# An encoder block on one core: attention is put into the same planned row of steps, and the same 51 buffers, as the rest

## The chip, the cores and the metric

The kernel runs on one core of a Trainium2 chip. The time is device microseconds of one execution. Five engines work side by side, each through its own instructions in order: PE (TensorE, matmuls; its weight loads are shown as PEld), DVE (VectorE), ACT (ScalarE), POOL (GpSimd) and SP (SyncE), which here issues nearly all DMAs. They wait for each other by semaphores.

## The reference, cut to what matters

One layer on x of 2048 tokens by 1024 features, all in float32:

```
h = rms_norm(x, norm1_g)
proj = h @ w_in                       # u, v | q, k, v | two gates of 1024
u, v = gelu(first 1024 columns)
y_a = u * (w_s @ layer_norm(v) + b_s)             # per chunk of 128 tokens, 4 groups
q, k = rms_norm(q, q_g) / 8, rms_norm(k, k_g)     # 8 heads of 64
# tokens are a grid of 32 rows x 64 columns; each query sees 8 rows x 16 columns
p = softmax(q . k_window + bias(na_rpb))
y_b = p @ v_window
merged = sigmoid(g1) * (y_a @ w_o_a) + sigmoid(g2) * (y_b @ w_o_b)
x = x + merged @ w_out
x = x + square(relu(rms_norm(x, norm2_g) @ w_ff1)) @ w_ff2
```

## The kernel before, in words

A float32 matmul is made of three fp32r matmuls: each operand is split into a high part (a cast on ACT, `t_hi`, `r_hi`, `w_hi`) and a low part (a subtraction on DVE, L1345, L1424). The large products go through a seven-product scheme (`seven` and `seven_tok`, L1452 and L682): sums of weight blocks are made on POOL (L1384 to L1391), sums of inputs on POOL too (`sums`, L415 to L428), and 7 steps of 12 matmuls of 128x512 replace 8.

The program has three parts, one behind the other, each with its own SBUF pool.

Part one, `first_steps` (L1054), is planned: `Plan` holds a list of PE steps and chains of stages on other engines (an SP load, a POOL sum, an ACT cast, a DVE subtraction, an SP store), each stage with a cost and a lead before the step that needs it. `Plan.run` goes through the steps once, keeps a model of each engine's clock and of 51 free buffers of 4 KB per partition, and writes every instruction in the order that it finds; the engines then follow this order. Part one makes u, the gates and then, in 16 slices of 128+128 tokens, v with the spatial gating (`values`, L701, 8 slices) and the queries and keys (`queries`, L822, 8 slices). What later steps need is stored to DRAM: `gt` (gates), `ut` (u), `ya`, `vs`, `qs`, `ks`. The input sums for the slices lie in DRAM as `xf`, laid out as [half, partition, 7 parts, 4, 512 tokens]; a slice reads 128 tokens of each, in runs of 512 bytes (L646). `bias_tables` (L977) builds the attention's bias in DRAM (`sk`, then nine tables `tb`) with DMAs and small operations on POOL; it is one chain, due at the end of part one.

Part two, attention (`attention`, L1243), is not planned: it is written out in program order with pools of its own, and a scheduler interleaves PE's work. There are 16 units (4 pairs of heads by 4 row blocks), each of 4 column blocks. For each of these 64 blocks PE makes the scores of two heads (L1177), DVE adds the bias and takes the maximum (L1184), ACT takes the exponential (L1187), DVE scales by the inverse sums (L1193), PE turns the result (L1206), DVE and ACT copy it (L1207, L1210), and PE multiplies by v (L1219). K is loaded from POOL's queue (`kst`, L1128), everything else from SP's. DVE reorders the queries (`q`, L1159). Between the blocks, 32 fillers (`branch_units`, L1276) multiply `ya` by w_o_a (L350, tiles `y`, `woa_hi`, `woa_lo`, `fg`), 12 matmuls of 128x512 each, times a gate `g` (L1306), stored as `ma`. Two fillers come ahead of attention, 24 within, 6 behind:

```
        with self.list_part():
            self.load_unit(0)
            units = self.branch_units()
            next(units)
            next(units)
```

Part three, `rest` (L1784), is planned by a second `Plan` with new buffers: the merge with w_o_b, w_out, and the two feed-forward products for each half of the tokens.

Of the kernel before, what the change touches and what calls it, by code (L numbers as in the profile page):

```python
# [19 lines left out]
P = 128  # L20
# [13 lines left out]
NRAW, NW, NACT, NBUF = 5, 12, 29, 51  # L34
# [209 lines left out]
class Block:  # L244


    def __init__(self, ctx, tc, a):
# [21 lines left out]
        self.xf = d("xf", [2, P, 7, 4, 512])  # L269
# [5 lines left out]

    def list_part(self):

        part = ExitStack()
        pool = lambda name, bufs: part.enter_context(self.tc.tile_pool(name=name, bufs=bufs, reuse_waits="tile"))
        self.slots = pool("slots", 1)  # L280
        self.half = pool("half", 5)
        self.ybp = pool("ybp", 1)
        return part
# [17 lines left out]
    def slot(self, shape, dt=F32, name="slot", tag="act"):  # L301
        return self.slots.tile([P] + shape, dt, tag=tag, name=name, bufs={"raw": NRAW, "w": NW, "act": NACT}[tag])

    def h512(self, dt=F32, name="half"):
        return self.half.tile([P, 512], dt, tag="half", name=name)

# [6 lines left out]

    def split(self, shape, src, name, pool=False):

        nc = self.nc
        hi = self.slot(shape, F32R, name + "_hi", "w")
        lo = self.slot(shape, F32R, name + "_lo", "w")
        if pool:
            nc.gpsimd.tensor_copy(hi, src)  # L320
            nc.gpsimd.tensor_tensor(lo, src, hi.bitcast(F32), ALU.subtract)
        else:
            nc.scalar.copy(hi, src)
            nc.vector.tensor_tensor(lo, src, hi.bitcast(F32), ALU.subtract)
        return hi, lo

    def load_raw(self, w, c0, ncol, nkt, name):

        per = 1024 // ncol
        raws = []  # L330
        for r0 in range(0, nkt * P, per * P):
            raw = self.slot([per, ncol], F32, name, "raw")
            self.nc.sync.dma_start(raw, w[r0 : r0 + per * P, c0 : c0 + ncol].rearrange("(k p) n -> p k n", p=P))
            raws.append(raw)
        return raws

    def load_wk(self, w, c0, ncol, nkt, name, pool=False):
        per = 1024 // ncol
        tiles = []
        for r0 in range(0, nkt * P, per * P):  # L340
            (raw,) = self.load_raw(w[r0 : r0 + per * P], c0, ncol, per, name)
            tiles.append(self.split([per, ncol], raw, name, pool))
        return lambda kt, hl: tiles[kt // per][hl][:, kt % per, :]
# [21 lines left out]
    def feat_gemm(self, w, m, X, nk=8):  # L365

        pt = self.ps("fg", "mm")
        ms = slice(m * P, (m + 1) * P)
        self.gemm(pt, [([w(k, 0)[:, ms], w(k, 1)[:, ms]], [X[k][:, 0], X[k][:, 1]]) for k in range(nk)])
        return pt  # L370


    def feat(self, h, xs, c0, row, act, dst, leads=(26, 15, 10)):
# [26 lines left out]
        for i, p in ((0, 2), (1, 4)):  # L400
            def out(i=i):
                nc.sync.dma_start(dst(i), e[i][1].rearrange("p b t -> p (b t)"))
                self.give(e[i][0])
            self.post(ids[p], [self.store(out, 1, 0)], 8)
# [44 lines left out]
    def norm_chain(self, e, name, i, k, acc, sq, after, width):  # L449
# [5 lines left out]
        def square():  # L455
# [4 lines left out]
            nc.scalar.activation(at(acc[0][1]) if k == 0 else at(sq[0][k % 2][1]), at(e[name][1]), AF.Square)  # L460
# [6 lines left out]
        return self.plan.chain([Stage("ACT", 0.1 + 0.5 * n, square, new, 0, 6, 0.3), Stage("DVE", 0.1 + 0.58 * n, add, 0, 0, 3, 0.3)], after)  # L467

    def first_u(self):
# [47 lines left out]
        for b in range(2):  # L517
# [47 lines left out]
            for _, st in fs:  # L565
                self.post(i, [self.store(st, 1, 0)], 2)
# [487 lines left out]
    def first_steps(self):  # L1054
# [28 lines left out]
        for c in range(2):  # L1083
            if c == 1:
                self.constants()
# [778 lines left out]
```

## Time and profile before

| what | value |
|---|---|
| median of 3 runs | 2811.0 us (2809.34 to 2811.19) |
| the profiled execution's own time | 2806.74 us |
| its span, first to last instruction | 2804.9 us |
| PE busy | 2561.2 us (91%) |
| DVE busy | 1857.1 us (66%) |
| ACT busy | 1159.6 us (41%) |
| POOL busy | 1105.1 us (39%) |
| mean granted clock of PE | 0.956 |
| DMA | 573.76 MB, mean 205 GB/s |

The span is the time of the program from its first to its last instruction; the runs' times hold about 2 us more. Busy shares are means over all stages. A table of stages (busy time of each engine, granted clock and DMA share in stretches of time) tells in which stages PE is not busy; the waits of that stage tell for whom. Stages of part one end near 880 us (start until 120, gates until 460, values until 640 and on to about 690, queries until 880), attention and its fillers run from 930 to 1231 us, and part three from there to the end.

### The profile page before, as it was taken

To read this page: it belongs to the slowest core of one execution; us is meant where nothing else is said; L and a number is where in the kernel's file an instruction comes from. 1 tells how busy PE (TensorE), PEld (TensorE's weight loads), DVE (VectorE), ACT (ScalarE), POOL (GpSimd) and SP (SyncE) were. 2 spreads that over 40 slices of the span, in tenths; PEclk is the share of its full clock that TensorE was granted. 3 is DMA by queue.
4 is the path that set the end of the run, shared out by engine and by line. 5 is a ranking of instruction groups with operands and counts; after the bars stand their busy time and mean duration, and the time that the engine had idled before them with its cause. 6 is when DMAs were issued, how large, how long until landed. Compare 5 with 4: busy or idle time off the path is not lost. (4 is left out here: it accounts for less than half of the span.)

```text
span 2804.9 us, 34089 instructions
## 1 busy us (share of the span) xinstructions
PE 2561.2 (91%) x11820; PEld 2071.9 (74%) x11820; DVE 1857.1 (66%) x2781; ACT 1159.6 (41%) x1802; POOL 1105.1 (39%) x800
## 2 busy tenths in 40 slices
PE   7799998779994799989998999989998999989999
PEld 5577887567773566668887888868886888868887
DVE  5667666547884477656376756588777666677776
ACT  5456545436542234423244443343333333443331
POOL 2553573540000111003334766634433666643441
PEclk9899999889997899999999999999999999989999
DMA  4467689989866999978766444474446444374442
GB/s 150 161 226 243 244 300 286 236 225 277 204 172 174 291 259 272 281 244 299 247 230 224 158 142 161 152 250 155 153 143 225 154 158 147 132 252 153 152 155 96
DMA packets 419164, 573.76 MB, mean 205 GB/s; under 512 B 33901, under 2 KB 283156, under 8 KB 418992
## 3 DMA queue, kind: packets, MB, share of 16 engines
q1 hardware_dynamic: 401600, 543.75, 60.8%
q0 software_dynamic: 13248, 27.82, 3.8%
q8 instruction: 93, 1.52, 0.2%
q10 hardware_dynamic: 4144, 0.02, 0.1%
q14 instruction: 79, 0.65, 0.1%
HBM read 368.45 MB, written 202.98 MB: 204 GB/s over the span
## 5 line engine op out<-in xcount | busy, mean ns | idle before, releaser
L1452 PE MATMUL z<-x_t,t_hi 128*128 128x512 f32 x1184 | 372.7, 396 | 39.4 <-DVE x L1768 28.2
L1345 DVE TENSOR_TENSOR r_lo<-w_r,r_hi 128x1024 fp32r<-128x1024 f32 (+3 forms) x176 | 286.3, 1628 | 82.0 <-ACT r_hi L1341 58.1
L1384 POOL TENSOR_TENSOR w_s<-w_r 128x512 f32<-128x512 f32 (+3 forms) x88 | 117.8, 1339 | 456.7 <-PE y L1452 261.2
L1452 PEld LDWEIGHTS z<-x_t,t_hi 128*128 128x128 f32 x1184 | 224.4, 191 | 92.2 <-DVE x L1768 10.3
L1452 PE MATMUL z<-x_t,t_lo 128*128 128x512 f32 x592 | 234.2, 396 | 1.5 <-DVE t_lo L1345 1.5
L1452 PE MATMUL x<-x_r,t_hl 128*128 128x512 f32 x888 | 219.7, 396 | 8.3 <-DVE x_r L1424 7.6
L1341 ACT CAST r_hi<-w_r 128x1024 fp32r<-128x1024 f32 (+3 forms) x176 | 173.7, 988 | 85.2 <-PE z L1452 62.7
L1452 PEld LDWEIGHTS x<-x_r,t_hl 128*128 128x128 f32 x888 | 169.9, 192 | 46.2 <-DVE x_r L1424 8.5
L1128 POOL DMA_DIRECT2D kst<-ks x32 | 26.5, 831 | 446.8 <-DMA ks<-qo 263.7
L1452 PE MATMUL z<-x_t,r_hi 128*128 128x512 f32 x592 | 183.6, 392 | 1.6 <-DVE x L1768 1.3
L1452 PE MATMUL z<-x_r,r_hi 128*128 128x512 f32 x592 | 183.9, 392 | 0.0
L1452 PE MATMUL y<-x_r,r_hi 128*128 128x512 f32 x592 | 183.6, 391 | 0.0
L1452 PE MATMUL x<-x_r,r_hi 128*128 128x512 f32 x592 | 182.2, 389 | 0.0
L1768 DVE TENSOR_TENSOR x<-z,x 128x512 f32<-128x512 f32 x152 | 104.8, 690 | 95.3 <-PE z L1452 95.3
L1420 ACT CAST x_r<-x_r 128x1024 fp32r<-128x1024 f32 x104 | 107.6, 1050 | 143.8 <-DVE t_hl L1345 99.9
L1391 POOL TENSOR_TENSOR w_s<-w_r,w_s 128x512 f32<-128x512 f32 (+3 forms) x88 | 151.3, 1719 | 37.0 <-DVE t_lo L1345 10.0
L1390 POOL TENSOR_TENSOR w_s<-w_r 128x512 f32<-128x512 f32 (+3 forms) x88 | 159.5, 1812 | 4.8
L350 PE MATMUL fg<-mg,w_hi 128*128 128x512 f32 x512 | 158.0, 389 | 0.9 <-DVE mg L1525 0.9
L1385 POOL TENSOR_TENSOR w_r<-w_r,w_r 128x512 f32<-128x512 f32 (+3 forms) x88 | 148.7, 1690 | 7.6 <-DMA w_r<-in_w_in_dram 0.6
L1345 DVE TENSOR_TENSOR t_lo<-w_s,t_hi 128x1024 fp32r<-128x1024 f32 (+3 forms) x88 | 136.2, 1548 | 16.6 <-ACT t_hi L1341 8.4
L1424 DVE TENSOR_TENSOR x_r<-x_r,x_r 128x1024 fp32r<-128x1024 f32 x104 | 138.7, 1352 | 3.5 <-ACT x_r L1420 3.5
L1420 ACT CAST x_t<-x_t 128x1024 fp32r<-128x1024 f32 (+1 forms) x104 | 84.6, 835 | 122.3 <-PE x L1452 80.6
(257 smaller groups left out, 6107.9 us busy)
## 6 DMA issues: line engine op xcount, KB each, us to landing
w_r<-in_w_ff_dram SPq DMA_DIRECT2D x116, 512.0 KB
x_r<-af SPq DMA_DIRECT2D x64, 512.0 KB
x_r<-xf SPq DMA_DIRECT2D x40, 512.0 KB
w_r<-in_w_in_dram SPq DMA_DIRECT2D x36, 512.0 KB
gt<-fe SPq DMA_DIRECT2D x32, 512.0 KB
qn<-qs SPq DMA_DIRECT2D x64, 256.0 KB
g<-gt SPq DMA_DIRECT2D x64, 256.0 KB
x<-x SPq DMA_DIRECT2D x32, 512.0 KB
```

The costliest lines, as they stand in the source:

```text
L350: self.nc.tensor.matmul(out, w[p], x[q], start=(i == 0 and j == 0), stop=(i == n - 1 and j == 2))
L1128: nc.gpsimd.dma_start(k.rearrange("p r c -> p (r c)"), self.ks[:, :, hd, pair, r0 * GW : (r0 + n) * GW].rearrange("l d t -> (l d) t"),)
L1341: nc.scalar.copy(e[name + "_"][1][0], e[name][1])
L1345: nc.vector.tensor_tensor(lo, e[name][1], hi.bitcast(F32), ALU.subtract)
L1384: nc.gpsimd.tensor_tensor(s23[:, :, 1], r1[:, :, 0], r1[:, :, 1], ALU.subtract)
L1385: nc.gpsimd.tensor_tensor(r1[:, :, 1], r1[:, :, 1], r2[:, :, 1], ALU.add)
L1390: nc.gpsimd.tensor_tensor(s23[:, :, 0], r1[:, :, 1], r1[:, :, 0], ALU.subtract)
L1391: nc.gpsimd.tensor_tensor(e["t4"][1], r2[:, :, 0], s23[:, :, 0], ALU.subtract)
L1420: nc.scalar.copy(hi, lo.bitcast(F32))
L1424: nc.vector.tensor_tensor(lo, lo.bitcast(F32), hi.bitcast(F32), ALU.subtract)
L1452: nc.tensor.matmul(out, a[u], b[v], start=(p in (1, 5, 2) and k == 0 and j == 0), stop=(k == n - 1 and j == 2), skip_group_check=p in (6, ...
L1768: nc.vector.tensor_tensor(v, bank, v, ALU.add)
```

## The change

All three parts become one plan. `list_part` and its pools go; `first_steps`, `attention` and `rest` add steps and chains to one `Plan`, with one set of 51 buffers, and `Plan.run` is called once. Attention's scores, turns and products are PE steps (`scores`, `turn`, `products`); block i's scores, then a filler if i is even, then block i-1's turn, then block i-2's products. Their loads are chains on SP, K's too. The query reorder is a POOL stage; the second head's scaling goes from DVE to ACT. The fillers go token block by token block with all of w_o_a held split (cast on ACT, subtraction on DVE) instead of column block by column block. Each load names the store that it comes after (`k_done`, `q_done`, `yb_done` and others). `bias_tables` starts behind the first steps and is due where the last gates begin. `xf` is laid out by token slices, so that a slice's two parts are one run of 4 KB; its stores and the second half's reload then go in runs of 512 bytes. The first 16 squares (`norm_chain`) go from ACT to POOL. Leads and costs of some stages get other numbers.

```diff
-        self.xf = d("xf", [2, P, 7, 4, 512])
+        self.xf = d("xf", [2, P, 4, 7, 4, P])
...
-            nc.scalar.activation(at(acc[0][1]) if k == 0 else at(sq[0][k % 2][1]), at(e[name][1]), AF.Square)
+            o, x = at(acc[0][1]) if k == 0 else at(sq[0][k % 2][1]), at(e[name][1])
+            if width == 512:
+                nc.gpsimd.tensor_tensor(o, x, x, ALU.mult)
+            else:
+                nc.scalar.activation(o, x, AF.Square)
...
-        return self.plan.chain([Stage("ACT", 0.1 + 0.5 * n, square, new, 0, 6, 0.3), Stage("DVE", 0.1 + 0.58 * n, add, 0, 0, 3, 0.3)], after)
+        return self.plan.chain([Stage("ACT" if n == 2 else "POOL", 1.3 if n == 1 else 1.1, square, new, 0, 6, 0.3), Stage("DVE", 0.1 + 0.58 * n, add, 0, 0, 3, 0.3)], after)
...
-        st += self.stores(e, ("w1", "w2", "t23", "t4"), self.xf[h][:, :, c], (True,) * 4)
+        def out(name, part):
+            def f():
+                p0, p1 = self.X_PART[part]
+                for p in range(p0, p1):
+                    v = e[name][1][:, p - p0] if p1 - p0 == 2 else e[name][1]
+                    nc.sync.dma_start(self.xf[h][:, :, p, c], v.rearrange("p (t q) -> p t q", q=P))
+                self.give(e[name][0])
+            return f
+
+        st += [Stage("SP", self.DMA, out(nm, p), 0, 1, 3 - 0.5 * i, 2.0) for i, (nm, p) in enumerate((("w1", "r1"), ("w2", "r2"), ("t23", "t23"), ("t4", "t4")))]
...
-                src = self.xf[h][:, p0:p1, :, t * P : (t + 1) * P] if n == 2 else self.xf[h][:, p0, :, t * P : (t + 1) * P]
+                src = self.xf[h][:, t, p0:p1] if n == 2 else self.xf[h][:, t, p0]
...
-            self.post(i, [self.store(out, 1, 0)], 6)
+            self.v_done[tok[0] // P] = self.v_done[tok[1] // P] = (self.post(i, [self.store(out, 1, 0, 5.0)], 6), 1)
...
+        start = len(plan.steps)
...
+            self.first_w(0, 2 + c, len(plan.steps) + 6)
...
-        plan.step(0.5, lambda: None)
-        end = plan.step(1.0, lambda: None)
-        self.bias_tables(mark, end)
-        plan.run()
...
+        self.bias_tables(start, end)
+
+
+    def unit(self, pair, rb):
+
+
+        nc, plan = self.nc, self.plan
...
+            def load_k(e=e, hd=hd):
+                e[0] = self.take([n, GW], F32R, "kst")
...
+            ks.append((e, plan.chain([Stage("SP", 1.6, load_k, 1, 0, 12, 3.0)], tuple(self.k_done[t] for t in rows), hold=(1, give))))
...
+            def order(e=e):
+                e[0] = self.take([4, 2, P], F32R, "q")
+                for cb in range(4):
+                    nc.gpsimd.tensor_copy(
+                        e[0][1][:, cb].rearrange("p l (r c) -> p (l r) c", c=16),
+                        e[1][1].rearrange("p l (r f c) -> p f (l r) c", f=4, c=16)[:, cb],
                     )
...
+            qs.append((e, plan.chain([Stage("SP", 1.8, load_q, 1, 0, 16, 3.0), Stage("POOL", 3.0, order, 1, 1, 6, 0.3)], tuple(self.q_done[t] for t in range(4 * rb, 4 * rb + 4)), hold=(1, give))))
...
+    def scores(self, pair, rb, cb, unit):
...
+        def first():
+            e["rec"] = self.sm(2, "rec")
+            nc.vector.reciprocal(e["rec"], e["sums"])
+            nc.vector.tensor_scalar(e["p"][1][:, 0], e["p"][1][:, 0], e["rec"][:, 0:1], None, ALU.mult)
+
+        def second():
+            nc.scalar.activation(e["p"][1][:, 1], e["p"][1][:, 1], AF.Copy, scale=e["rec"][:, 1:2])
...
+        i = plan.step(0.95 * u, prod, [c for _, c in ks + qs] + [bias[1]], evac, 1, {"DVE": 1.15 * u, "ACT": 0.8 * u})
+        ch = plan.chain([Stage("DVE", 0.15 + 0.5 * u, first, 0, 0, 1.5, 0.2), Stage("ACT", 0.1 + 0.5 * u, second, 0, 0, 0.8, 0.2)], start=i)
...
+        fills = self.branch_units()
+        done = 0
...
+                p[i] = self.scores(*todo[u], cb, units[u])
+            while done < 32 and done * 64 <= 32 * i:
+                next(fills)
+                done += 1
...
+                pT[i - 1] = self.turn(todo[u][1], cb, p.pop(i - 1))
...
+                s = self.products(todo[u][1], cb, units[u], pT.pop(i - 2), po, o)
...
+                ys.append((e, plan.chain([self.load(e, "y", [2, 512], self.ya[:, :, k, b * 512 : b * 512 + 512], 8, dt=F32R)],
+                                         tuple(self.ya_done[t] for t in range(4 * b, 4 * b + 4)), hold=(1, lambda e=e: self.give(e["y"][0])))))
...
+                    g = plan.chain([self.load(e, "g", [512], self.gt[at], 8)], (self.gt_done[b // 2, m],))
+                    i = plan.step(12 * self.MM, prod, [ws[c][1], g] + [y[1] for y in ys], evac, 0, {"DVE": 0.7})
+                    self.ma_done[m, b] = (self.post(i, [self.store(out, 1, 0, 1.0)], 6), 1)
...
-    def w_seven(self, w, k1, k2, c0, leads=(26, 15, 10)):
+    def w_seven(self, w, k1, k2, c0, leads=(22, 14, 9)):
...
-                [Stage("SP", self.DMA * n / 2, load, 1, 0, 14, 3.0),
+                [Stage("SP", self.DMA * n / 2, load, 1, 0, 11, 3.0),
...
-        with self.plan_part("one"), self.tc.manual_schedule():
+        with self.plan_part("buf"), self.tc.manual_schedule():
             self.first_steps()
-        with self.list_part():
-            self.units, self.bias = {}, {}
-            self.load_unit(0)
-            units = self.branch_units()
-            next(units)
-            next(units)
-            done = 2
-
-            def fill(step):
-                nonlocal done
-                while done < 26 and done < 2 + (step + 1) * 24 / 64:
-                    next(units)
-                    done += 1
-
-            self.att_queries(self.units[0])
-            self.attention(fill)
-            for _ in units:
-                pass
-        with self.plan_part("two"), self.tc.manual_schedule():
+            self.attention()
             self.rest()
```

The places where the order of instructions changes most are shown below as they stand in the two programs, without row numbers; names carry the buffer's number.

PE before, where the queries end and attention begins: `qT` turns the last slice's queries and keys, `fg` is a filler, `s` are scores.

```order
L893 MATMUL qT_6848<-ident_98,q_6626 128x128 x4
L893 MATMUL qT_6856<-ident_98,k_6666 128x128 x4
L350 MATMUL fg_6963<-y_6915,woa_hi_6949 128x512 x2
L350 MATMUL fg_6963<-y_6915,woa_lo_6950 128x512
...
L350 MATMUL fg_6980<-y_6921,woa_lo_6950 128x512
L350 MATMUL fg_7116<-y_6923,woa_hi_6949 128x512 x2
L350 MATMUL fg_7116<-y_6923,woa_lo_6950 128x512
L350 MATMUL fg_7116<-y_6925,woa_hi_6949 128x512 x2
L1177 MATMUL s_7008<-kst_6889,q_6995 128x264 x2
```

PE after, at the same place (L851 is the turn, L1154 the scores, L304 the filler, L1199 the turn of p):

```order
L851 MATMUL qT_6928<-ident_98,q_6676 128x128 x4
L851 MATMUL qT_6943<-ident_98,k_6721 128x128 x4
L1154 MATMUL s_6955<-kst_6635,q_6557 128x264 x2
L1154 MATMUL s_6958<-kst_6637,q_6694 128x264 x2
L304 MATMUL fg_6984<-y_6824,w_hi_6530 128x512 x2
L304 MATMUL fg_6984<-y_6824,w_lo_6531 128x512
...
L1154 MATMUL s_6998<-kst_6635,q_6557 128x352 x2
L1154 MATMUL s_7001<-kst_6637,q_6694 128x352 x2
L1199 MATMUL pTp_7015<-ident_98,p_6961 120x128 x2
```

Two whole fillers stood ahead of the first scores; now one filler stands behind them, and steps are whole groups.

SP before, behind the last stores of the queries (`qs`, `ks`); `woa` is the fillers' first weight load:

```order
L917 DMA qs_72<-qo_6853 64x8x128 x2
L915 DMA ks_73<-qo_6861 64x4x128 x4
L1135 DMA qn_6891<-qs_72 64x2x512 x2
...
L1118 DMA bias_6913<-tb20_88 128x2x264
L1284 DMA y_6915<-ya_79 128x2x512
L1284 DMA y_6917<-ya_79 128x2x512
```

SP after, there:

```order
L604 DMA x_t4_6407<-xf_93 128x512
L1369 DMA w_6409<-in_w_o_a_dram 128x4x256
L875 DMA qs_72<-qo_6425 64x8x128 x2
L1096 DMA qn_6507<-qs_72 64x2x512 x2
L873 DMA ks_73<-qo_6467 64x4x128 x4
L875 DMA qs_72<-qo_6510 64x8x128 x2
L873 DMA ks_73<-qo_6539 64x4x128 x4
L1096 DMA qn_6611<-qs_72 64x2x512 x2
L1084 DMA kst_6635<-ks_73 128x704
```

Before, all of the first unit's loads and then 16 loads of `y` stood behind the last store and ahead of `woa`; now the weights, queries and keys of the first unit stand among the stores of the last slices, and four `y` follow.

POOL before, where the bias tables follow the last sums of part one:

```order
L1391 TENSOR_TENSOR w_s4_3128<-w_r2_3030,w_s23_3106 128x512
...
L428 TENSOR_TENSOR t4_3242<-w2_3134,t23_3223 128x512
L987 MEMSET rpbv_3374 120x96
L988 DMA rpbv_3374<-in_na_rpb_dram 120x31
L991 DMA sk_81<-rpbv_3374 1920x1x96
L999 DMA cmask_3378<-in_column_mask_dram 128x96
L1015 DMA tbt_3413<-sk_81 16x15x24 x8
```

POOL after, in the gates: the same DMAs stand between the weight sums (L1394 to L1401):

```order
L950 DMA sk_81<-tbx_755 1920x1x96
L957 DMA tbx_755<-in_column_mask_dram 128x96
L364 TENSOR_TENSOR t23_798<-w1_627 128x512
...
L973 DMA tbx_755<-sk_81 16x15x24 x8
L978 TENSOR_TENSOR tbx_755<-tbx_755 128x360
...
L989 DMA tb02_84<-tbi_913 8x16x288
L1394 TENSOR_TENSOR w_s23_956<-w_r1_894 128x4x128
L1395 TENSOR_TENSOR w_r1_894<-w_r1_894,w_r2_896 128x4x128
```

Before, nothing of the gates stood behind the tables; now each sum stands behind some of their DMAs.

## Rows read from the trace of the kernel before

**Rows 1.** Stages: us; busy (count) of PE, PEld, DVE, ACT, POOL; clock, DMA share, GB/s.
```profile
0.00:120.00 120.00, 83.91 (x329) 66.45 (x330) 75.96 (x85) 65.01 (x91) 54.38 (x42) 0.87 0.44 140
120.00:460.00 340.00, 328.11 (x1430) 267.73 (x1428) 216.36 (x223) 175.19 (x232) 179.33 (x116) 0.98 0.74 256
460.00:640.00 180.00, 133.37 (x575) 108.55 (x576) 99.47 (x161) 78.34 (x105) 78.25 (x130) 0.88 0.93 242
640.00:880.00 240.00, 220.51 (x1025) 177.30 (x1024) 203.17 (x462) 124.68 (x204) 0.00 (x0) 0.98 0.73 193
880.00:930.00 50.00, 1.44 (x4) 0.50 (x2) 1.50 (x2) 2.06 (x3) 4.45 (x4) 0.50 1.03 318
930.00:1231.00 301.00, 283.43 (x1886) 210.95 (x1886) 210.44 (x743) 124.64 (x392) 35.74 (x37) 0.94 0.93 256
1231.00:1260.00 29.00, 15.73 (x58) 12.00 (x57) 6.43 (x8) 3.13 (x4) 3.81 (x3) 0.76 0.96 337
1260.00:2804.00 1544.00, 1494.69 (x6522) 1228.45 (x6520) 1043.78 (x1100) 586.53 (x773) 749.10 (x470) 0.98 0.53 179
```

**Rows 2.** Waits from 870 to 950 us: us in total, times, longest.
```profile
PE fg L350 <- POOL woa_hi L320: 47.5, 1, 47.5
POOL woa_hi L320 <- DMA woa<-in_w_o_a_dram: 42.0, 1, 42.0
```

**Rows 3.** Timeline of SP's issues ahead of the first weight load: start, us, what.
```profile
898.48 15.89 SPq L1284 DMA_DIRECT2D y<-ya  x16
```

**Rows 4.** Waits of PE from 1195 to 1260 us.
```profile
PE fg L350 <- ACT w_hi L1341: 13.2, 1, 13.2
```

**Rows 5.** Waits from 455 to 645 us, in the values.
```profile
ACT ya L793 <- DMA vs<-av: 27.1, 4, 14.0
PE z L682 <- ACT vg L714: 25.0, 4, 9.7
PE z L682 <- DVE av L726: 20.1, 3, 11.5
```

**Rows 6.** Timeline of PE, one slice of values to the next.
```profile
650.03 1.05 PE L782 MATMUL mix<-spc,vg 128*128 128x128 f32 x8
670.88 1.05 PE L782 MATMUL mix<-spc,vg 128*128 128x128 f32 x8
```

**Rows 7.** Timeline of PE, one slice of queries to the next.
```profile
792.89 0.63 PE L893 MATMUL qT<-ident,k 128*128 128x128 f32 x4 [0.66 <-DVE k L876]
814.92 0.63 PE L893 MATMUL qT<-ident,k 128*128 128x128 f32 x4 [0.65 <-DVE k L876]
```

**Rows 8.** Three stretches of 40 us, columns as in the first group.
```profile
960.00:1000.00 40.00, 40.00 (x288) 30.96 (x287) 30.93 (x108) 19.77 (x58) 4.36 (x4) 1.00 1.00 251
1240.00:1280.00 40.00, 35.36 (x144) 28.57 (x145) 22.35 (x25) 12.02 (x16) 16.62 (x11) 0.88 1.06 379
480.00:520.00 40.00, 36.77 (x170) 30.21 (x168) 23.44 (x39) 20.50 (x28) 22.24 (x37) 0.99 0.99 241
```

**Rows 9.** Timeline of PE in attention: scores, a turn, products.
```profile
1211.15 0.98 PE L1177 MATMUL s<-kst,q 128*128 128x384 f32 x4
1211.98 0.82 PE L1206 MATMUL pTp<-ident,p 128*120 128x128 f32 x6
...
1220.62 1.68 PE L1219 MATMUL pv<-pT,vw 128*64 128x128 f32 x24
```

**Rows 10.** DVE by line from 930 to 1232 us: busy, mean ns.
```profile
L1159 DVE CAST q<-qn 128x256 fp32r<-128x256 f32 x128 | 32.1, 315 | 0.0
```

**Rows 11.** Timeline of the start: the same sum on DVE beside a POOL sum, and alone.
```profile
26.30 1.92 POOL L1384 TENSOR_TENSOR w_s<-w_r 128x512 f32<-128x512 f32 x1 [25.00 <-DMA w_r<-in_w_in_dram]
26.98 3.49 DVE L464 TENSOR_TENSOR acc<-acc,sq 128x512 f32<-128x512 f32 x2
...
55.13 0.68 DVE L464 TENSOR_TENSOR acc<-acc,sq 128x512 f32<-128x512 f32 x1
```

**Rows 12.** Waits of POOL from 440 to 640 us, in the bias tables.
```profile
POOL tb L1029 <- DMA tb<-tbi: 23.9, 24, 2.7
POOL tbt L1015 <- DMA sk<-rpbv: 12.6, 1, 12.6
```

More of the change, by code (lines that the diff above doesn't have):

```diff
@@ L362, in rsqrt, with feat @@
         nc.vector.tensor_tensor(r, r, t2, ALU.mult)
[L365 to L373, printed above, removed]
+    def feat(self, h, xs, c0, row, act, dst, done, leads=(22, 14, 9)):
         nc, plan = self.nc, self.plan
@@ new lines, in unit, with load_b @@
+        if rb != 2:
+            kind = ROWBLK[rb][2]
+            for ct in range(3):
+                e = {}
+                def load_b(e=e, ct=ct, kind=kind):
+                    w = KIND_N[kind] * KIND_W[ct]
+                    e[0] = self.take([2, w], F32, "bias")
+                    src = self.tb[ct][kind][2 * pair : 2 * pair + 2].rearrange("h r c k -> (r c) h k")
+                    nc.sync.dma_start(e[0][1], src)
+                give = lambda e=e: self.give(e[0][0])
+                self.bias[pair, ct, kind] = (e, plan.chain([Stage("SP", 1.6, load_b, 1, 0, 10, 3.0)], (self.bias_done,), hold=(1, give)))
@@ new lines, in turn, with products, prod, evac @@
+        plan.step(0.14 * 2 * -(-n // per), prod, [p[1]], evac, 1, {"DVE": 0.75, "ACT": 0.8}, 1)
+        return e
+    def products(self, rb, cb, unit, pT, po, o):
+        nc, plan = self.nc, self.plan
+        n, w = ROWBLK[rb][1], COLBLK[cb][1]
+        per = P // w
+        vt = unit[2][cb // 2]
+        def prod():
+            if cb % 2 == 0:
+                po[0] = self.ps("pv", "pv")[:, :256]
+            for j in range(0, n, per):
+                m = min(per, n - j) * w
+                for hd in range(2):
+                    nc.tensor.matmul(
+                        po[0][hd * HD : (hd + 1) * HD, cb % 2 * P : (cb % 2 + 1) * P],
+                        vt[0][0][1][:m, cb % 2, j // per, hd * HD : (hd + 1) * HD],
+                        pT[0][1][:m, hd, j // per, :],
+                        start=(j == 0),
+                        stop=(j + per >= n),
+                    )
+        def evac():
+            self.give(pT[0][0])
+            if cb == 0:
+                o[0] = self.take([2, 512], F32R, "yb")
+            if cb % 2:
+                c2 = cb // 2
+                src = po[0].rearrange("p (f r c) -> p f r c", f=2, c=16)
+                hi, lo = (o[0][1][:, l].rearrange("p (r f c) -> p f r c", f=4, c=16)[:, 2 * c2 : 2 * c2 + 2] for l in (0, 1))
+                nc.scalar.copy(hi, src)
+                nc.vector.tensor_tensor(lo, src, hi.bitcast(F32), ALU.subtract)
+        return plan.step(0.14 * 2 * -(-n // per), prod, [vt[1]], evac, int(cb == 0), {"DVE": 0.5, "ACT": 0.5} if cb % 2 else {}, 1)
@@ L1286, in branch_units @@
[L1286 to L1308 removed]
+                e = {}
```

399 lines of the change are left out of this document (163 added, 236 removed).

## The prediction

> **What bounds the kernel now.** I read the table of stages first, then the waits of the stages with holes, then the timeline at their edges. In the table [rows 1] PE is the engine that sets the time: busy 97% in the gates and in part three, where its clock was granted at 0.98. The losses sit in five places. The reader is to see: the start, 36 us idle at clock 0.87; the values, 47 us idle in 180 at clock 0.88 with a DMA share of 0.93; a stretch of 50 us between queries and attention with 1.44 us of PE work; attention, hardly idle but at clock 0.94 and DMA share 0.93; and 29 us around the start of part three with 15.7 us of work at clock 0.76.
>
> The waits name the causes. Between queries and attention PE waits 47.5 us for the split weights of the first filler, and POOL, which splits them, 42.0 us for their load [rows 2]; SP issues that load behind 16 loads of y that alone take 15.9 us to issue [rows 3], and all of them behind the last store of the queries. At the second edge PE waits 13.2 us for the first weights of the new plan [rows 4]. In the values PE waits for ACT and DVE, 25.0 and 20.1 us, but ACT itself stands for stores of vs to land before buffers come free, 27.1 us [rows 5]: with DMAs at 0.93 everything that passes through them is late, and the engines' orders carry it to PE.
>
> **The change part by part.** The sum is made against the profiled execution, 2806.7 us: its span of 2804.9 and 1.8 around it. The median of the runs is 4.3 us above it, and I add that at the end.
>
> *Edge to attention.* The first weights, queries and keys of the first unit now stand on SP among the stores of the last slices, and only four y ahead of the first gate load. The first unit needs rows 0 to 10, the first half's slices, which were stored long before. So the wait of 47.5 us goes. What is late next is the first exponentials and scalings, with one filler to cover them; I leave 5.5 us. Term: -42. At most it is -47.5; at least -30, if the first loads queue behind the stores for as long as y's took.
>
> *Attention.* It took 301 us for 1886 matmuls. PE's own work: the undisturbed stretch did 288 in 40 us at full clock [rows 8], so 1886/288 x 40 = 262 us. A second way: scores 0.98 x 371/384 columns, a turn 0.82 x 6.5/6, products 1.68 x 13/24 [rows 9] make 2.75 us for each of 64 blocks, and 32 fillers at 12 x 0.225 us (part three: 1494.69 us x 0.98 for 6522 matmuls [rows 1]) make 86: 262 again. The next group starts some 0.15 us ahead of the end of the last (1211.98 against 1211.15 + 0.98), so whole groups could come down to 262 - 64 x 3 x 0.15 = 233. The clock of 0.94 on 301 us is 18 us of today's loss, and comes from holes at the changes of unit. DVE is not the bound after: of 210 us it loses 32 for the query order [rows 10] and half of the scaling. That order on POOL is not in the trace: between DVE's 0.32 us and POOL's longest sum in these rows, 1.92 us [rows 11], 8 of them are 2.5 to 15 us per unit of 17 us, on an engine with 36 us of work in 301; it hides, and would be the bound only at the upper end. I take the nearer, 0.4. But the DMA share of 0.93 stays, and 12 of the 16 loads of y now fall into the stage. I add 12 us of late loads to 262: 274. Term: -27, between -56 (245) and +25 (the rival below).
>
> *Values and queries.* Undisturbed slices take 20.85 us for values [rows 6] and 22.03 for queries [rows 7]: 8 of each are 343 us; from 460 to 880 it took 420. Of the 77 us, I leave 12, what the gates, planned in the same way with DMAs at 0.74, stand idle. The relief: the bias tables, 12.45 MB by the code, go elsewhere; and a slice's 1.835 MB come in runs of 4 KB. A stretch rich in 512-byte runs moved 241 GB/s at a share of 0.99, that is 243 at a full one; one rich in long runs 379 at 1.06, that is 358 [rows 8]. So the tables are 51 us of DMA time and a slice falls from 7.5 to 5.1. Of 0.93 x 180 = 167 us, 51 and 8 x 2.4 = 19 go: 97 us, a share of 0.6. Term: -65, between -77 and -15.
>
> *Gates.* Here those 51 us arrive, and 22 MB of xf stores and reloads turn to short runs, 22 x (1/243 - 1/358) = 29 us more. Today's 0.74 x 340 = 252 us become 332 of 340 by these prices, a share of 0.98; with the tables at the gates' own rate (256/0.74 = 346 GB/s, 36 us) and the runs free it is 288, 0.85. POOL's row gets the tables between the weight sums: they were its 78 us of work from 460 to 640 [rows 1], and 23.9 and 12.6 us of waits for their own DMAs [rows 12], 115 us in all, beside 179 us of sums in 340. It fits, with sums late at times. The first load of the tables (12.6 us of waiting) has four sums between it and the next one now, so half of it is covered. At the rate of 460 to 640 us, where 26% stood idle, it would cost 88 us; at that of the gates today nothing. Weights are asked for 22 planned us ahead, slices only 16, so I stay near the gates' own row: +12.
>
> By a rule of the Trainium skill (DMA: Bandwidth & Descriptors, Specifications), transfers of 512 bytes and more run at line rate, so the new layout neither helps the slices nor hurts the stores. The trace does not agree: 243 against 358 GB/s at a full share. By the rule the gates' term would be near 0 and the time 2663.
>
> *Start.* 16 squares leave ACT for POOL. A sum on DVE took 1.75 us while POOL summed and 0.68 alone [rows 11]. If each square slows one DVE operation, that is 16 x 1.07 = 17 us on an engine that is busy 76 of 120 us; as the stage also has holes that ACT's relief may close, the ends are -5 and +17, and I take +4.
>
> The Trainium skill (SBUF — State Buffer, SBUF: two separate sides) has it that GpSimd and a VectorE operation with two SBUF inputs lock each other out of a shared port for a whole instruction. The row agrees, 1.75 against 0.68. Counted in full the time would be 2688.
>
> *Second edge.* The 13.2 us go, and with them most of the low clock around it (29 us at 0.76 is 7 us): the loads of the merge now stand among attention's last stores, and the y it needs first come from units two earlier. I leave 2 us. Term: -18.
>
> *Part three.* Same work; leads of loads 14 to 11, of weights 26 to 22, of x1 8 to 5. It idles 49 us in 1544, at the edges between the feed-forward products. 0, with 10 to either side.
>
> Sum: -42 - 27 - 65 + 12 + 4 - 18 = -136; 2806.7 - 136 = 2670.7, and 4.3 for the median: **2675 us**.
>
> **The rivals.** *Attention is bound by its transfers.* For: a share of 0.93 to 1.00 throughout, at 256 GB/s. Its 301 us moved 77 MB; 6 MB of y come in: 83 MB at 256 GB/s are 326 us instead of 274, a time of 2727. Against: other stretches moved 379, and K's loads leave the POOL queue.
>
> *The values are not relieved.* For: the waits named are ACT's and DVE's, and the loads are now planned closer. If only 15 of 77 us come back, 2725. Against: gates planned alike, with a lower DMA share, lose 12 in 340.
>
> *Slower: POOL's order in the gates.* The 115 us of tables lie ahead of weight sums that PE waits for. Laid bare in full, with the clock that falls in holes (in the values 47 us idle cost 0.12 x 180 = 22 more, 0.47 per us), they cost 115 x 1.47 = 169 instead of 12: 2832. It decides from about 100 us laid bare (148 us, the 136 gained and the 12 counted). Against: POOL has 161 us free there.
>
> *The plan gives nothing*: waits stay in number and only change names; 2811. Against it: the edge of 47.5 us is no wait that a neighbour can take over.
>
> **How the numbers follow.** Forecast 0.68; attention bound by transfers 0.14; values not relieved 0.09; both 0.02 (2777); slower 0.05; nothing 0.02. What a measurement here tells from no change is 0.2%, about 6 us. So faster 0.93, same 0.02, slower 0.05. The range: all good ends of the terms together make 2608, and I stop at 2615; upward it takes in both single rivals and most of the gates' bad end (2675 + 76 = 2751): 2750. The forecast's own range is 2615 to 2715.
>
> **What would show it.** Right: no stretch of 40 us with PE under 30 behind the gates; the values' period near 21 us and their DMA share near 0.6; attention from first to last scores in 260 to 290 us, the first of them within 10 us of the last query's turn; the gates idle 15 to 30 us of 340. Wrong: PE waits in attention that end with a DMA of q, k, v or bias at a share of 1.0 (first rival); slices longer than 24 us (second); POOL sums that start late behind L989, with PE waiting for L1355 (third). The forecast fails if the gates grow by over 60 us or attention stays above 310.

## The result, and the profile after

The changed kernel takes 2721.9 us (2714.4 to 2722.6) against 2811.0: a ratio of 0.9677, 95% interval 0.965 to 0.9703. The forecast was 2675, the range 2615 to 2750. The sign and the range held; the point was 47 us too low.

Stages of the changed kernel, in the columns of [rows 1]. The bounds are its own stages: start, gates, values, queries, attention, the edge to part three, part three.

```profile
0.00:81.00 81.00, 53.77 (x216) 42.55 (x216) 54.09 (x61) 39.71 (x51) 53.56 (x44) 0.91 0.48 150
81.00:489.00 408.00, 363.19 (x1542) 295.36 (x1542) 247.12 (x247) 192.83 (x257) 277.65 (x260) 0.94 0.81 253
489.00:690.00 201.00, 185.70 (x850) 153.54 (x850) 153.34 (x247) 122.88 (x164) 0.00 (x0) 0.96 0.79 250
690.00:869.00 179.00, 162.38 (x752) 128.48 (x751) 151.55 (x378) 82.05 (x147) 3.41 (x10) 0.98 0.73 197
869.00:1152.00 283.00, 261.05 (x1900) 204.28 (x1900) 175.58 (x558) 159.26 (x462) 45.27 (x119) 0.99 1.06 319
1152.00:1199.00 47.00, 43.48 (x183) 34.65 (x182) 30.13 (x33) 15.36 (x21) 24.25 (x15) 0.96 1.01 360
1199.00:2712.00 1513.00, 1465.80 (x6384) 1204.51 (x6382) 1019.59 (x1073) 573.10 (x755) 732.08 (x458) 0.98 0.52 176
```

The reader is to see two stages. Attention's DMA share is 1.06, higher than before (0.93), while PE is busy 92% of it. The gates, 97% busy before, are now 89% busy at a clock of 0.94. Measured from marker to marker (first gate matmul, first token slice, last transpose of the queries, first product of `w_out`) the terms are these:

| term | predicted | measured |
|---|---|---|
| start | +4 | -5.3 (86.5 to 81.2) |
| gates, with the two U products | +12 | +34.3 (373.1 to 407.4) |
| values and queries | -65 | -40.3 (420.6 to 380.3) |
| edge to attention | -42 | -47.8 (47.5 to -0.3) |
| attention, first scores or fillers to the last of either | -27 | -23.3 (303.7 to 280.4) |
| second edge, from there to the first product of `w_out` | -18 | -9.9 (59.6 to 49.7) |
| part three, from there to the end | 0 | 0 (1513.9 and 1513.9) |
| span | -136 | -92.3 (2804.9 to 2712.6) |

The first edge behaved as the prediction had it: the wait of 47.5 us [rows 2] has no successor, and PE's first scores start at 868.6 us, before the last transpose of the queries ends. At the second edge 3.5 us of waiting for `yb` stand where 13.2 for weights stood [rows 4].

What PE waits for in the gates (before, 86 to 460 us, its waits for ACT's copies; then after, 81 to 500 us): us in total, times, longest.

```profile
PE z L1452 <- ACT fe L384: 9.3, 5, 3.9
```
```profile
PE z L1467 <- ACT fe L330: 41.6, 10, 13.5
PE z L1467 <- DVE z L493: 12.4, 1, 12.4
PE z L640 <- DVE x_r L616: 3.2, 1, 3.2
```

L330 (L384 before) is the copy by which ACT empties a bank of PSUM, the memory that PE's sums go to; PE waits for it before it uses the bank again. These waits grew by 32.3 us, about what the stage grew. Why the copy was late by 13.5 us the timeline of ACT shows (start, us, operation, and in brackets the idle time before it with its cause):

```profile
322.56 0.62 ACT L1351 CAST t_hl<-w_s 128x512 fp32r<-128x512 f32 x1 [3.44 <-POOL t L374]
332.53 2.38 ACT L556 ACTIVATE w<-w,g 128x1024 f32<-128x1024 f32 x2 [9.35 <-DMA w<-in_xT_dram]
334.82 0.57 ACT L330 COPY fe<-z 128x512 f32<-128x512 f32 x1
```

and the timeline of SP its loads:

```profile
322.94 1.03 SPq L1388 DMA_DIRECT2D w_r<-in_w_in_dram  x2
324.07 1.82 SPq L1369 DMA_DIRECT2D w<-in_xT_dram  x2
```

The copy was ready to run. It stood in ACT's fixed order behind the scaling of two rows of xT (L556), whose loads SP issued only at 324. It is not POOL's weight sums, the place that the slower rival named, but the rows that `rows_out` makes: the change had cut their lead from 26 planned us to 16 (the diff in the part on the change leaves this line out).

That is the longest of the ten waits. In the next two ACT stood for another transfer in front of its copies: for a load of token operands (8.8 us of PE's time, at 280 us) and for a store of a gate to land (6.6, at 118). What ACT waits for in the stage (81 to 490 us), the three that are transfers:

```profile
ACT w L556 <- DMA w<-in_xT_dram: 12.4, 6, 9.3
ACT fe L330 <- DMA gt<-fe: 7.1, 1, 7.1
ACT x_r L1435 <- DMA x_r<-xf: 5.4, 2, 4.6
```

In attention PE's longest waits end with transfers, 15.5 us of the stage (the wait for `yb` falls at 1155, behind it):

```profile
PE pv L1226 <- DMA vw<-vs: 7.8, 8, 2.9
PE fg L304 <- DMA y<-ya: 5.9, 10, 1.1
PE fg L304 <- DMA y<-yb: 3.5, 1, 3.5
PE s L1154 <- DMA kst<-ks: 1.8, 3, 0.8
```

In values and queries the middle is undisturbed; the losses sit at the first slices, where the split weights arrive, and at the last transposes of the queries:

```profile
480.00:520.00 40.00, 29.99 (x116) 23.79 (x115) 31.43 (x33) 24.46 (x31) 6.40 (x5) 0.87 1.00 375
520.00:640.00 120.00, 120.00 (x579) 101.11 (x578) 87.67 (x155) 70.67 (x95) 0.00 (x0) 1.00 0.69 202
840.00:880.00 40.00, 31.35 (x145) 24.55 (x146) 31.05 (x89) 17.11 (x38) 2.88 (x8) 0.87 0.93 259
```

### The profile page after: what moved, and what is told of

The parts are those of the page before. It is cut to its first block, busy times and chain, and to the rows that moved or that the text cites. A ratio compares the mean times of both kernels' runs of the same rounds, so it can differ in the third digit from the quotient of the medians.

```text
span 2712.6 us, 34217 instructions
## 1 busy us (share of the span) xinstructions
PE 2535.4 (93%) x11820; PEld 2063.4 (76%) x11820; DVE 1831.4 (68%) x2593; ACT 1185.2 (44%) x1854; POOL 1136.2 (42%) x904
## 3 DMA queue, kind: packets, MB, share of 16 engines
q8 instruction: 93, 1.52, 0.2%
## 4 chain that ended last, share of the span: by engine, by line
PE 70%; DMA 11%; DVE 7%; issue 3%; POOL 3%; ACT 2%; SPq 1%; DVEq 0%; POOLq 0%; ACTq 0%
PE z L1467 28%; PE x L1467 13%; PE fg L304 11%; PE y L1467 7%; PE z L640 4%; PE x L640 2%; DMA vw<-vs 1%; PE y L640 1%; PE s L1154 1%; DMA w<-in_xT_dram 1%; PE pv L1226 1%; PE pTp L1199 1%; DMA kst<-ks 1%; DVE x_r L1439 1%; DMA bias<-tb 1%
## 5 line engine op out<-in xcount | busy, mean ns | idle before, releaser
L1355 DVE TENSOR_TENSOR r_lo<-w_r,r_hi 128x1024 fp32r<-128x1024 f32 (+3 forms) x176 | 280.9, 1597 | 107.3 <-ACT r_hi L1351 102.8
L1394 POOL TENSOR_TENSOR w_s<-w_r 128x512 f32<-128x512 f32 (+3 forms) x88 | 152.6, 1734 | 396.0 <-DVE x L1784 164.4
L1101 POOL CAST q<-qn 128x256 fp32r<-128x256 f32 x128 | 48.7, 423 | 588.6 <-DMA ks<-qo 337.9
L304 PE MATMUL fg<-y,w_hi 128*128 128x512 f32 x512 | 162.2, 398 | 9.4 <-DMA y<-ya 5.9
L1400 POOL TENSOR_TENSOR w_s<-w_r 128x512 f32<-128x512 f32 (+3 forms) x88 | 162.3, 1844 | 3.4
L304 PE MATMUL fg<-mg,w_hi 128*128 128x512 f32 x512 | 158.0, 389 | 0.8 <-DVE mg L1540 0.8
L1401 POOL TENSOR_TENSOR w_s<-w_r,w_s 128x512 f32<-128x512 f32 (+3 forms) x88 | 143.0, 1625 | 27.4 <-DVE r_lo L1355 11.1
L1355 DVE TENSOR_TENSOR t_lo<-w_s,t_hi 128x1024 fp32r<-128x1024 f32 (+3 forms) x88 | 135.1, 1535 | 17.3 <-ACT t_hi L1351 8.3
L1467 PEld LDWEIGHTS z<-x_t,r_hi 128*128 128x128 f32 x592 | 112.0, 190 | 30.2 <-issue 4.8
```

Of the source, the lines that this page charges most:

```text
L304: self.nc.tensor.matmul(out, w[p], x[q], start=(i == 0 and j == 0), stop=(i == n - 1 and j == 2))
L1101: nc.gpsimd.tensor_copy(e[0][1][:, cb].rearrange("p l (r c) -> p (l r) c", c=16), e[1][1].rearrange("p l (r f c) -> p f (l r) c", f=4, c=1 ...
L1355: nc.vector.tensor_tensor(lo, e[name][1], hi.bitcast(F32), ALU.subtract)
L1394: nc.gpsimd.tensor_tensor(s23[:, :, 1], r1[:, :, 0], r1[:, :, 1], ALU.subtract)
L1400: nc.gpsimd.tensor_tensor(s23[:, :, 0], r1[:, :, 1], r1[:, :, 0], ALU.subtract)
L1401: nc.gpsimd.tensor_tensor(e["t4"][1], r2[:, :, 0], s23[:, :, 0], ALU.subtract)
```

## The experiments

Times are medians; stage lengths come from one profiled execution each, between the markers of the table. The gates of six kernels whose program is the same up to there (the first experiment and five built on it) lie between 380 and 389 us, so a difference of under 8 us in that stage shows nothing by itself.

### The rows' lead (e1)

```
- load of xT rows in rows_out: lead 16     ACT scale: lead 13
+ load of xT rows in rows_out: lead 26     ACT scale: lead 16
```

> The changed kernel, but the rows of xT in the gates are asked for 26 planned us ahead and scaled 16 ahead, as before the change (it has 16 and 13). Theory A (the gates grew by 34 us because ACT, in its fixed order, stands at a scaling whose row has not landed, and the copies that free PE's banks stand behind it): the waits of PE for ACT's copies in the gates fall from about 57 us to under 30, gates 385 to 397 us instead of 407, time 2702 to 2712. Theory B (the tables' transfers and POOL work fill the gates): gates 404 to 410, time 2719 to 2725.

Measured: 2695.2 us (2691.3 to 2696.9), ratio 0.9582 (0.9564 to 0.9601); the gates 385.8 us. PE's waits for ACT's copies fell from 41.6 to 10.3 us:

```profile
PE z L1467 <- ACT fe L330: 10.3, 9, 2.0
```

Theory A holds: the short lead cost 21.6 us of gates, more than the 13.5 of the one wait whose cause the timeline shows. No wait for ACT's copies is longer than 2.0 us now: those at 118 and 280 us went too, and in what way the rows' lead did that no run shows. At 385.8 the gates are 12.7 above before, the +12 that the prediction had set for the tables alone.

### The tables' place, with the short lead (e2) and the long one (e12)

```
- self.bias_tables(start, end)              # beside the gates
+ self.bias_tables(mark, len(plan.steps) - 1)   # from the second U product on
```

> The changed kernel, but the bias tables are made from the second U product on and are due at the last query step, as before the change. Theory A (late rows of xT are what the gates lost, the tables cost them little; the tables' removal is what relieved values and queries): gates 399 to 407 us, values and queries 405 to 420 instead of 380, time 2740 to 2760. Theory B (the tables are what the gates lost): gates 375 to 385 us, values and queries 395 to 415, time 2712 to 2730.

> The kernel with the longer lead for the rows of xT (2695 us, query tiles loaded twice), and the bias tables made from the second U product on, as before the change. Theory (the lead matters only where the tables fill the queue; they cost the gates about 10 us once the rows are early): gates 372 to 378 us, values and queries 415 to 424, time 2714 to 2726, like the late tables with the short lead (2720). Rival (the short lead cost 20 us by itself): gates 352 to 360 us, time 2695 to 2705.

Measured, with the changed kernel and e1 beside them:

| tables, lead of the rows | gates | values and queries | time |
|---|---|---|---|
| beside the gates, 16 (the change) | 407.4 | 380.3 | 2721.9 |
| beside the gates, 26 (e1) | 385.8 | 383.7 | 2695.2 |
| late, 16 (e2) | 375.2 | 420.0 | 2719.7 (2718.0 to 2734.6) |
| late, 26 (e12) | 373.1 | 425.1 | 2724.5 (2722.0 to 2727.7) |

For e2 each theory had half: the gates lose their tables' cost as B said (375), the values lose their relief as A said (420). e12 decides between the readings: without the tables the lead is worth nothing (373.1 against 375.2). So the two act together: with the tables beside the gates a lead of 26 is enough, one of 16 is not. By what the tables make the rows late (the shared DMA engines, or POOL's sums behind the tables' DMAs) no run separates. And the tables' departure is the whole gain of values and queries, 40 of 40 us.

### Long or short runs (e3, e11)

```
- xf [2, P, 4, 7, 4, P]    # a slice of 128 tokens in long runs
+ xf [2, P, 7, 4, 512]     # stored in runs of 2 KB, sliced in runs of 512 bytes
```

> The changed kernel, but the token rows are stored as before the change, in runs of 2 KB, so that slices of 128 tokens are read in runs of 512 bytes. By the prices of the prediction (243 against 358 GB/s at a full share): the slice's 1.835 MB go from 5.1 to 7.5 us, DMA share in the values 520 to 640 up from 0.69 to about 0.8; values and queries 385 to 400 us instead of 380; the gates get 10 to 29 us of DMA time back and come out at 385 to 405 us; time 2710 to 2735. Rival (runs of 512 bytes and more cost the same): both stages and the share stay within 4 us and 0.03, time 2719 to 2725.

Measured: 2718.2 us (2712.4 to 2724.8), ratio 0.9668 (0.9646 to 0.969); gates 403.8, values and queries 382.5. The same stretch of the values as above, now with short runs:

```profile
520.00:640.00 120.00, 120.00 (x579) 101.09 (x578) 88.37 (x157) 69.17 (x94) 0.00 (x0) 1.00 0.78 206
```

The share rose from 0.69 to 0.78, about 1.9 us of DMA time for a slice of 20.85 us (the prediction said 2.4). The packets of the same two stretches, long runs first:

```profile
DMA packets 23810, 24.19 MB, mean 202 GB/s; under 512 B 2038, under 2 KB 18281, under 8 KB 23802
DMA packets 42012, 24.70 MB, mean 206 GB/s; under 512 B 2064, under 2 KB 39315, under 8 KB 42003
```

So the price was nearly right, and bought nothing: PE is busy throughout in both. By the Trainium skill (DMA: Bandwidth & Descriptors, Specifications), transfers from 512 bytes on run at line rate. The share does not agree with it, 0.78 against 0.69 for nearly the same bytes; the time tests nothing here, as PE had no gap.

> The same kernel as the one with the three products at the end of the queries, but with the token rows in runs of 2 KB, sliced in runs of 512 bytes, as before the change. If the layout of the rows buys nothing even where the rows have their lead: within 5 us of its time, at a share of DMA time in the undisturbed values of 0.78 instead of 0.70 and in the gates 0.04 lower. If the long runs only could not show their worth because the gates were held by the late rows: 6 to 15 us slower. If their short stores held the gates: 5 to 10 us faster.

Measured: 2671.3 us (2669.6 to 2674.9) against the 2668.1 of e9 below, on the same chip, within the 5 us that were set for no difference; nor do the gates differ (384.1 and 382.4; their DMA share from 81 to 465 us is 0.80 with 2 KB stores, 0.87 with long slices, 27 us of DMA time where the prediction priced 29). The share of the undisturbed values is 0.79 against 0.74. Values and queries took 389.4 us against 383.8, and 381.5 to 386.3 in e1, e5, e6 and e7, which differ there at most in attention's first loads, so a few us in favour of the long runs are not excluded. Where the rows have their lead the layout is worth little as well.

### The squares (e4)

```
- nc.gpsimd.tensor_tensor(o, x, x, ALU.mult)
+ nc.scalar.activation(o, x, AF.Square)
```

> The changed kernel, but the 16 squares of the start are made on ACT as before the change. If ACT's relief is what made the start 5 us shorter than before: first gate matmul at 84 to 88 us instead of 81, time 2724 to 2729. If POOL's squares cost DVE time through the port (1.07 us each, as the prediction priced it): first gate matmul at 74 to 80, time 2710 to 2720. If neither matters: 80 to 82, 2719 to 2725.

Measured: 2728.0 us (2722.2 to 2732.0), ratio 0.97 (0.9678 to 0.9722); first gate matmul at 85.5 us instead of 81.2 (79.8 to 82.8 in the other eleven experiments). DVE operations in the start, first with the squares on POOL, then on ACT (columns: count, busy us, mean ns, idle before):

```profile
L444 DVE SCALAR_TENSOR_TENSOR r<-w,g,r 128x512 fp32r<-128x512 f32 x16 | 16.3, 1066 | 6.5 <-ACT r L440 6.5
L414 DVE TENSOR_TENSOR acc<-acc,sq 128x512 f32<-128x512 f32 x14 | 14.4, 1036 | 1.2 <-POOL sq L408 0.9
```
```profile
L411 DVE TENSOR_TENSOR acc<-acc,sq 128x512 f32<-128x512 f32 x14 | 12.7, 909 | 1.5 <-ACT sq L407 0.9
L441 DVE SCALAR_TENSOR_TENSOR r<-w,g,r 128x512 fp32r<-128x512 f32 x16 | 12.3, 809 | 7.2 <-ACT r L437 7.2
```

DVE does pay, 4.0 and 1.7 us in these two groups, a third of the 17 that the prediction priced at most. The price of one operation was near, 0.8 us against 1.07, but their number was not: of these 30 operations of the changed kernel eight began while a square ran, and took 1.51 to 1.56 us each. The three beside which a square began later took 0.69 to 0.74, like those with no work on POOL beside them (0.68 to 0.75). One that began beside a square and one alone, from DVE's timeline:

```profile
24.14 1.52 DVE L414 TENSOR_TENSOR acc<-acc,sq 128x512 f32<-128x512 f32 x1
31.73 0.68 DVE L414 TENSOR_TENSOR acc<-acc,sq 128x512 f32<-128x512 f32 x1
```

ACT is relieved by 9.0 us (48.93 to 39.90 busy before the first gate matmul), and that weighs more. The end of the range that the prediction gave for ACT's relief, -5, is what came.

### What bounds attention (e5, e6, e7)

All three stand on e1. e5 loads each query tile once and lets POOL copy it to both halves:

```
  ...
- for dup in range(2):
-     dma_start(qn[dup * HD : (dup + 1) * HD], qs[...])
+ dma_start(qn[:HD], qs[...])
  ...
  for cb in range(4):
-     gpsimd.tensor_copy(q[:, cb], qn[...])
+     for dup in range(2):
+         gpsimd.tensor_copy(q[dup * HD : (dup + 1) * HD, cb], qn[:HD ...])
```

> The kernel with the longer lead for the rows of xT (2695 us), and in attention each query tile is loaded once, into 64 partitions, and POOL's ordering copies it to both halves (8 copies of 64 partitions for 4 of 128): 7.3 MB of 89 MB less from attention's first to its last product. Theory A (transfers at a share of 1.06 bound attention): 283 us come down by the bytes, to 260 to 268, time 2673 to 2683. Theory B (the order of PE, ACT and DVE bounds it): 279 to 285 us at a lower DMA share, time 2691 to 2699. If POOL's ordering, doubled from 46 to about 92 us, becomes the wait: PE waits for q, over 287 us.

e6 adds a transfer in each unit, a copy from memory to memory: `+ dma_start(xx[u], xT[128 rows, 1024 columns])`.

> The kernel with the longer lead for the rows of xT, and in attention each of the 16 units also copies 0.5 MB of xT to memory that nobody reads (8.4 MB more, 9%). Theory A (transfers bound attention): 283 us become 300 to 312, time 2712 to 2724. Theory B (the order bounds it, the share of 1.06 is only a busy queue): 281 to 288 us, time 2693 to 2701.

e7 changes leads alone: keys 12 to 16, values 10 to 15, y 8 to 13, biases 10 to 12.

> The kernel with the longer lead for the rows of xT, and attention's loads are asked for earlier: keys 16 planned us ahead instead of 12, values 15 instead of 10, y 13 instead of 8, biases 12 instead of 10. Theory A (transfers bound attention): 280 to 286 us, other waits in place of those for vw and y, time 2692 to 2699. Theory B (loads are only asked for too late, PE's waits for vw, y and kst are 13.5 us): 266 to 274 us, time 2678 to 2687.

Measured: e5 2674.0 us (2664.7 to 2675.7), ratio 0.9516 (0.9494 to 0.9539); e6 2717.2 (2715.5 to 2724.7); e7 2714.0 (2704.7 to 2717.0). Attention from first scores to last product, in e5, e1, e6 and e7:

```profile
855.00:1116.00 261.00, 252.06 (x1887) 200.78 (x1886) 174.78 (x557) 158.65 (x461) 99.01 (x240) 1.00 1.06 316
```
```profile
850.00:1132.00 282.00, 259.29 (x1886) 203.67 (x1884) 174.74 (x557) 159.14 (x462) 46.21 (x120) 0.98 1.06 316
```
```profile
848.00:1153.00 305.00, 268.41 (x1888) 209.75 (x1888) 175.82 (x557) 159.99 (x462) 45.96 (x120) 0.94 1.05 318
```
```profile
841.00:1142.00 301.00, 268.15 (x1890) 208.05 (x1890) 175.19 (x557) 160.10 (x462) 45.49 (x120) 0.95 1.04 296
```

Length times rate gives 82, 89 and 97 MB at 316 to 318 GB/s: the stage is as long as its bytes. Theory A holds in both directions, 21 us less and 23 us more. POOL's ordering, doubled to 99 us, is no wait. In e5 PE is busy 252 of the 261 us, so little is left there for fewer bytes to give. e7 is a miss for both theories: with the same 89 MB it took 301 us. The loads that were moved ahead have gone past others on SP, and those are late now:

```profile
DVE g L1309 <- DMA g<-gt: 31.4, 9, 5.6
```

That was 5.0 us in e1. The copies of the transposed probabilities stand behind it on DVE, ACT waits for these 55.2 us (22.9 in e1), and PE for ACT's 23.3 (1.8). Why the rate itself fell to 296 at a share of 1.04 no run shows.

### The token operands' lead (e8)

```
- Stage("SP", DMA * n / 2, load, 1, 0, 11, 3.0)    # in x_seven
+ Stage("SP", DMA * n / 2, load, 1, 0, 14, 3.0)
```

> The kernel with the longer lead for the rows of xT, and the token operands and the split weights of the values and queries are asked for 14 planned us ahead, as before the change, instead of 11. If short leads are what else the gates lost (PE waits 8.5 us for x_r and x_t in the stage, at the change from gates to U, where the clock falls to 0.80): gates 373 to 380 us instead of 386, values and queries 378 to 383 instead of 384, time 2682 to 2690. If the queue is full there in any case (share 1.01): within 4 us of 2695.

Measured: 2700.5 us (2694.5 to 2708.8), ratio 0.962 (0.9593 to 0.9647), no gain over e1, on which it stands, and outside both expectations. Values and queries came down to 375.5, the gates went up to 393.0. In the last 35 us of the gates ACT stands for a store to land before its buffer is free, at a DMA share of 1.02:

```profile
ACT r_hi L1351 <- DMA gt<-fe: 12.0, 1, 12.0
```

What one stage won the other paid, 8 and 7 us against e1. With the tokens' lead back the gates were not shorter, so it is no cause of their loss, the rows' is; the weights' lead (26 to 22) was not tried alone.

### Work for the end of the queries (e9)

This stands on e5.

```
  ...
  while self.todo:
-     plan.step(0.5, lambda: None)
+     next(self.fills)             # a product of w_o_a
      self.between()
```

> The kernel that loads each query tile once (2674 us), and three products of the branch's output projection stand between the last four transposes of the queries, where three empty steps of the plan stood; attention gets three fewer. Theory: PE's wait of 7.2 us for DVE at the last transposes of the queries is covered, and attention does not miss the fillers, since its transfers bound it: from the last value product to the merge 6 to 10 us less, time 2663 to 2669. Rival: the fillers' y and weights now queue among the last query stores, and PE waits for them, or attention's first exponentials lie bare: 2672 to 2680.

Measured: 2668.1 us (2666.3 to 2676.2), ratio 0.9497 (0.9477 to 0.9516). The time is the one forecast, but not by the reason given: from the last product of the query slices to the first product of `w_out` it took 320.0 us (834.3 to 1154.3), in e5 319.2 (844.6 to 1163.8). The wait of 7.2 us went and nothing was gained; the share of 1.04 in the 320 us fits that the bytes of attention still set the length. The 6 us lie in the gates (382.4 against 388.6), within the spread of equal programs. So this edit is not shown to gain; the kernel with e1, e5 and e9 is the fastest here, 54 us under the changed one, and e5 without e9 stands at 48.

### The bytes of the tables alone (e10)

This too stands on e5.

```
+ 24 times beside the first six slices: dma_start(xx[u], xT[128 rows, 1024 columns])
```

> The kernel that loads each query tile once, and beside the first six slices of the values 24 copies of 0.5 MB of xT to memory that nobody reads, 12.6 MB on SP's queue, about the bytes of the bias tables but none of their work on POOL. Theory (the bytes are what the tables cost there): values and queries 411 to 425 us instead of 386, time 2699 to 2713. Rival (POOL's own queue, its waits or its descriptors were the cost, the bytes fit beside the slices): 386 to 394 us, time 2674 to 2682.

Measured: 2679.3 us (2674.2 to 2679.9), ratio 0.9526 (0.9508 to 0.9544); values and queries 393.5 us against 386.3 in e5 and 383.8 in e9. 12.6 MB more cost 7 to 10 us there; the late tables cost 40 (e2 against the change) and 41 (e12 against e1). DMA queues in the values with the late tables (e2, 458 to 640 us: packets, MB, share of the 16 engines):

```profile
q1 hardware_dynamic: 27157, 31.90, 56.8%
q0 software_dynamic: 8611, 13.91, 31.6%
```

On POOL's queue 13.91 MB took 0.316 x 182 = 57.5 us of all engines' time, 242 GB/s; SP's 31.90 MB in 103 us ran at 309. So the rival holds for the larger part: it isn't the bytes. The copies match the tables in bytes but not in DMA time: SP's queue, with them in it, moved its bytes at 322 GB/s of its own time (470 to 640 us of e10, 48.17 MB at 88.0%). So whether the cost is the tables' DMA time on POOL's queue, their short rows, or POOL's work beside DVE stays open.

## Why the prediction was right in sign and 47 us off

In the span the sum is 44 us short: the gates lack 22, values and queries 25, the second edge 8 and attention 4, while the start gave 9 and the first edge 6 more than forecast. The other 3 us are the median, which lies 7.5 us above the profiled execution instead of 4.3.

**The edges.** The first was right: the loads could move ahead, nothing took the place of the 47.5 us, and the term came within 6 us. At the second, -9.9 instead of -18, the 13.2 went, but a wait of 3.5 for `yb` came, and the low clock that the prediction took off with them, 7 us, gave nothing back: from the merge's first matmul to `w_out`, without that wait, it took 46.4 us before and 46.3 after.

**Gates, +12: the sum left out a term.** The prediction had the shorter leads in front of it ("weights are asked for 22 planned us ahead, slices only 16"; it did not name the rows that `rows_out` loads, also 16) and used them to choose a price for the tables. It did not price what stands behind a late row on ACT. With the rows' lead restored the term is +12.7, and e12, which has the lead but not the tables, is at the 373.1 of before. POOL's order, which it watched instead, was no wait: PE's waits for split weights were under 2 us. Its sign for that ("PE waiting for L1355") rightly stayed silent, and the sign "gates idle 15 to 30 us" rightly failed, with 45.

**Values and queries, -65: a term mis-sized.** It measured -40.3. The step that failed is the conversion of DMA time into time: 51 us for the tables' bytes and 19 for the runs were to bring the stage to 12 us of loss. The tables' departure brought 40 (e2, e12), the runs nothing clear of noise (e3, e11). And the 40 are not the price of bytes: as many of them, added as plain copies, cost only 7 to 10 us (e10). The share in the values fell to 0.79, not 0.6; their middle runs without a gap, and 380.3 - 343 = 37 us stay at the ends: the weights' arrival, the change to queries, the last transposes. The truth lay between the forecast (65 us back) and the second rival (15).

**Attention, -27: near the number, by the wrong reason.** PE's own 262 us plus 12 for late loads made 274; it took 280. The sign set for being right, first to last scores in 260 to 290 us, held with 274.5, by luck, since another limit gave the number. The stage is bound by bytes: the first rival's mechanism, shown by e5 and e6, and by its sign, PE's waits for `vw` and `kst` at a full share. The rival's time was wrong because it took the 256 GB/s of before [rows 1] for the limit; the stage now moves 316 to 319. That 256 came at a share of 0.93: brought to a full share, as the prediction did with its other rates, it is 275 and gives 303 us. Why the rate rose further was not tried.

**Start, +4: the wrong sign.** DVE's loss is a third of the price, since half as many operations met a square as were counted; ACT's relief outweighs it (e4).

**Part three, 0:** right.

The 2663 that the prediction gave for runs whose length costs nothing takes their price out of the gates alone; the values' term held 19 us of the same price, so that time was too low.

The time lies 7 us above the forecast's own range (2615 to 2715) and within the one that takes in the rivals. Two mechanisms of the prediction fell: that long runs buy time, and that PE bounds attention.

## What to carry to other kernels

When transfers move into a stage, look at every in-order engine for an operation that waits for a load and has PSUM evacuations behind it: such a load's lead is what pays, and it is cheap to give back (21.6 us here). In a stage whose length is its bytes divided by one rate, taking bytes away shortened it here (21 us for 7 MB), while longer leads for some of its loads made others late (18 us more). DMA time saved where PE has no gap is worth nothing, so price it only where a wait ends with that transfer.

## What was not expected of the hardware

Attention moved 316 to 318 GB/s in three kernels with 82, 89 and 97 MB, at shares of 1.05 and 1.06; the next stage moved 358 to 360 at 1.00 to 1.01. A full share is therefore not one rate. The mean packet differs in the same sense: 1.26 KB in attention (e1: 89.17 MB in 70689 packets) and 1.61 KB in the next stage (16.91 MB in 10525), and where e3 made the packets smaller, the share for the same bytes rose. That this alone sets the rate is not shown. An operation of DVE that began while POOL squared took 1.52 us instead of 0.68, nearly as much longer as beside POOL's sums (1.75 in [rows 11]), and one that had begun before the square took no longer (e4); the means of the groups, 1036 and 1066 ns, hide both. POOL ordered 64 partitions in 395 ns and 128 in 403 (medians), so copying to both halves doubled its time and cost attention nothing.
